# Tying the output product's sums further back, a second partial-sum buffer, and other buffers for the first pair's parts

## The chip, the core and the metric

The kernel runs on one core of a Trainium2 chip. The metric is the device time of one launch in microseconds (us). Five engines work from their own instruction queues: PE (TensorE, the matmuls), ACT (ScalarE), DVE (VectorE), POOL (GpSimd) and SP (SyncE, which here only starts DMAs). The instructions of an engine run in the order in which the program holds them; between engines, semaphores make one wait for another.

## The reference

One decoder block in fp32 on 512 tokens and 16 meta tokens, width 1024: a retention branch and a gated linear-recurrence branch, merged by sigmoid gates, and then a SwiGLU feed-forward part. The change touches the feed-forward part and what shares its helpers:

```python
u = rmsnorm(h, ffn_norm_w[l])
gu = u @ w_ffn_in[l]                      # 1024 x 5632
g, up = gu[..., :FFN_HIDDEN], gu[..., FFN_HIDDEN:]
h = h + (jax.nn.silu(g) * up) @ w_ffn_out[l]   # 2816 x 1024
h = rmsnorm(h, final_norm_w)
```

## The kernel before

**Operands in two parts.** PE multiplies a rounded fp32 type, so each fp32 operand is split into a high part (a cast on ACT) and a low part (source minus high part, on DVE), and each product is three matmuls: high by high, high by low, low by high (lines L431 to L433, or L441 to L443 with 256 columns). For a weight piece of 128x512, `emit` makes the two parts: the cast is L350 (L348 with a sign), the subtraction L356. They live in a ring of 9 buffers, so a piece can be made up to 9 pieces ahead of its use. For an activation `split` does the same (L497 on ACT, L498 on DVE).

**Seven products for eight.** Most products are done in blocks by Winograd's scheme: seven block products of sums and differences of the operands' quarters in place of eight. `fast` and `fast512` do one tile of 128 output columns in that way. They use two PSUM banks, in the trace `zwf` (z and w) and `yxf` (y and x) in the feed-forward part. After the first products of a tile, partial sums are copied out: `ws` (L465, ACT), the second half of `pz` (DVE), the first half of `pz` (L467, ACT); the last product of `yxf`, with the weight sum s2, is added into the bank which L467 has read; then `u2` (L474, ACT) copies the bank and two DVE additions write the tile's output. `pz` has one buffer for each name, so a tile's copy waits for the tile before to have read its own.

**The feed-forward part.** Twenty tiles j = 2 to 21 of `w_fi` (the first two are done in another way ahead of them) give silu(g)*up in 11 pairs of hidden blocks, kept in `F[i]`. `VX` holds the parts of the seven activation operands (t1, t3, b21, b11, ...); at its last use in the last tile, `last_use` gives back an operand's two buffers to `slots`, a list from which `get` takes the one that has been free longest. When the last tile has used t3, `first_parts(0)` starts the output product's first operand.

**The output product** (`fo` in the trace, eight accumulators `acc`, one in each PSUM bank) takes pairs 0 to 8 in two stages, since eight banks hold four of the products at a time. The first stage runs t1, t3, b11, b21 of each pair, 24 matmuls with 512 columns; before each pair's products `first_parts` forms a difference `ab[i]` (L1395, DVE) and splits it and a half of `F[i]`, four casts and subtractions of 128x512. At its end four banks are added out to SBUF (`add_to`, L1490, DVE). The second stage runs t2, b22, t4 of each pair, 18 matmuls. Its operands are begun by `begin_second`: the 128x256 difference L1408, its split, and the difference L1411, all in `F[i]`'s and `ab[i]`'s buffers; `second_parts` splits the other half. The weight sums of t1 and t2 are made in `emit` on DVE (L335 and L337); t3 and t4 come by an adding DMA. Two pairs without Winograd's scheme (9 and 10) fill in after pairs 2 and 5 and end the product, with 48 matmuls at the end; the norm and the writing of the output follow.

**What sets the order.** A scheduler puts the instructions of each engine in an order by its own estimate of when each can start, and the order then is fixed. `behind(ins, other)` adds a dependency that only fixes that ins stands after other on their engine, without a semaphore. `in_turn` ties an addition to the latest low part of a weight (`state["low"]`), and `split(..., held=True)` ties its cast and its subtraction to the latest high and low part, so that an addition can't go ahead of the weights that were emitted before it in the text.

Of the kernel before, what the change touches and what calls it, by code (L numbers as in the profile page):

```python
# [10 lines left out]
F32 = mybir.dt.float32  # L11
F32R = mybir.dt.float32r
# [5 lines left out]
P = 128  # L18
# [37 lines left out]
EARLY = (2, 5)  # L56
BY_DMA = 20
LEAD = 2

ON_POOL = {"w_out": (1, 3)}  # L60
Z_POOL = False
# [96 lines left out]
def hybrid_block(ctx: ExitStack, tc: tile.TileContext, a: dict):  # L158
# [96 lines left out]
    def behind(ins, other):  # L255

        if other is not None:
            tc.add_manual_dep(ins.ins, other.ins.name, mybir.DependencyInfo(
                mybir.DependencyClass.NoSync, mybir.DependencyReason.DATA), reason="issue order")
        return ins  # L260

    def in_turn(ins):
        return behind(ins, state["low"])

    kept = {}
    loaded = {}
# [28 lines left out]
    def emit(n, later=False):  # L295
# [34 lines left out]
        if key == "w_fo" and isinstance(c, str):  # L330
            b11, b12, b21 = (lambda q=q: quarter(key, i, q) for q in (2, 0, 3))
            b22 = lambda: quarter(key, i, 1)
            if c == "t1":
                tb[i] = get(Q4)
                in_turn(nc.vector.tensor_tensor(tb[i], b12(), b11(), op=ALU.add))  # L335
            elif c == "t2":
                in_turn(nc.vector.tensor_tensor(tb[i], tb[i], b22(), op=ALU.add))  # L337
            src = {"t1": lambda: tb[i], "t2": lambda: tb[i], "t4": lambda: tb[i], "t3": lambda: sums[key, i, "t3"],
                   "b11": b11, "b21": b21, "b22": b22}[c]()
        elif c in ("s1", "s2", "s3", "s4"):  # L340
            src = sums[key, i, c]
        else:
            src = quarter(key, i, {"a21": 0, "a22": 1, "a11": 2, "a12": 3}.get(c, c))
# [1 line left out]
        lo = wpool.tile([P, Q4], F32R, tag="lo", bufs=RING, name=f"lo{n}")  # L345
        turned = key == "w_fo" and c == "b11"
        if turned:
            state["high"] = nc.scalar.activation(hi, src, AF.Copy, scale=-1.0)  # L348
        else:
            state["high"] = nc.scalar.copy(hi, src)  # L350
        loaded[pieces[n]] = hi, lo

        def low(engine):
# [6 lines left out]
        if on_pool(key, i, c):  # L360
            low(nc.gpsimd)
        else:
            state["low"] = low(nc.vector)
        if key == "w_fo" and c == "t2":
            add_quarter(tb[i], key, i, 3)
        if key == "w_fo" and c == "t4":
# [79 lines left out]
    def fast(key, s, X, n, banks, name, used):  # L446

        z, w_, y, x = banks
        own = n == TH
        ws = small.tile([P, TH], F32, tag="ws", name=f"ws{name}{s}")
        pz = small.tile([P, 2, TH], F32, tag="pz", name=f"pz{name}{s}")
        u2 = small.tile([P, TH], F32, tag="u2", name=f"u2{name}{s}")
        part = lambda name: weights((key, s, name))[0]
        block(z, part("s1"), X["t1"], n, True)
        used("t1")
        block(w_, part("s3"), X["t3"], n, own)
        used("t3")  # L460
        block(y, part("a12"), X["b21"], n, True)
        used("b21")
        block(x, part("a11"), X["b11"], n, own)
        used("b11")
        nc.scalar.copy(ws[:, :n], w_)  # L465
        nc.vector.tensor_tensor(pz[:, 1, :n], z, ws[:, :n], op=ALU.add)
        nc.scalar.copy(pz[:, 0, :n], x)  # L467
        block(z, part("s4"), X["b22"], n, False)
        used("b22")
        block(w_, part("a22"), X["t4"], n, False)  # L470
        used("t4")
        block(x, part("s2"), X["t2"], n, False)
        used("t2")
        nc.scalar.copy(u2[:, :n], x)  # L474
        return pz, u2
# [19 lines left out]
    def split(p, src, engine=nc.vector, held=False):  # L495
        hi, lo = p
        high = nc.scalar.copy(hi, src)  # L497
        low = engine.tensor_tensor(lo, src, hi.bitcast(F32), op=ALU.subtract)  # L498
        if held:
            behind(high, state["high"])  # L500
            behind(low, state["low"])


    class Pair:
# [883 lines left out]
    def first_parts(i):  # L1388

        if i >= SEVEN or i in parts:  # L1390
            return
        f = F[i]
        ab[i] = get(512)
        by_tile = f.rearrange("p (k n) -> p k n", k=2)
        in_turn(nc.vector.tensor_tensor(ab[i].rearrange("p (k n) -> p k n", k=2), f[:, :512].rearrange("p (k n) -> p k n", k=2),  # L1395
                                by_tile[:, :, 256:], op=ALU.subtract))
        parts[i] = get(D, F32R), get(D, F32R)
        split([p[:, 512:1024] for p in parts[i]], ab[i])
        split([p[:, :512].rearrange("p (k n) -> p k n", k=2) for p in parts[i]], by_tile[:, :, :256], held=True)

# [2 lines left out]
    def begin_second(i):  # L1403

        if i >= SEVEN or i in s2:
            return
        f, t = F[i], ab[i][:, :256]
        in_turn(nc.vector.tensor_tensor(t, f[:, :256], ab[i][:, 256:], op=ALU.subtract))  # L1408
        s2[i] = get(512, F32R)
        split((s2[i][:, :256], s2[i][:, 256:]), t)  # L1410
        nc.vector.tensor_tensor(f[:, 512:768], f[:, 512:768], t, op=ALU.subtract)  # L1411
        put(ab.pop(i))
# [12 lines left out]

    def last_use(b):
        put(*VX.pop(b))
        if b == "t3":
            first_parts(0)

    for j in range(FIRST, NJ):
        gu = get(D)
# [184 lines left out]
```

## Time and profile before

| | |
|---|---|
| three runs | 914.54, 915.37, 916.05 us (median 915.37) |
| the profiled execution | 914.75 us, its span 913.0 us |
| PE busy | 893.9 us of the span (98%), 6506 matmuls |
| DVE busy | 716.3 us (78%) |
| ACT busy | 489.9 us (54%) |
| granted TensorE clock, mean of the span | 0.995 |
| last matmul ends | about 905.3 us after the span's start |

The span is the time from the first to the last instruction of the profiled execution, on whose clock all times below lie. In the timeline a row holds the start, the duration, engine and line, the operation with output and inputs, how many instructions of one kind stand in the row, and in brackets how long the engine had been idle before it and what released it. A matmul's duration overlaps the next one's; the spacing of two starts is what it costs.

### The profile page before, as it was taken

What the parts mean: (1) busy time and instruction counts of PE and PEld (TensorE: products, weight loads), DVE (VectorE), ACT (ScalarE), POOL (GpSimd) and SP (SyncE); (2) the same over time, 40 slices, a digit from 0 to 9 for tenths busy, and PEclk for the clock granted to TensorE, in tenths of its full rate; (3) what the DMA queues carried; (4) which work ended last, traced back from release to release, by engine and by line L of the source; (5) the groups of instructions that cost most, each with busy time, mean ns of one, the idle gap of its engine ahead of it and who ended that gap; (6) DMA issues with size and microseconds to landing.
All of it is one profiled execution on the core that took longest, in us unless ns stands there. A gap on an engine that the chain in (4) does not pass through costs nothing.

```text
span 913.0 us, 17003 instructions
## 1 busy us (share of the span) xinstructions
PE 893.9 (98%) x6506; PEld 843.0 (92%) x6506; DVE 716.3 (78%) x1197; ACT 489.9 (54%) x877; POOL 87.2 (10%) x101
## 2 busy tenths in 40 slices
PE   8999999999999999999999999999999999998996
PEld 7999999999999889999998888999999999886775
DVE  5999978987888738868745427989999997898982
ACT  6655545554466246857833325555565565564553
POOL 3200000000100011211200220000000001101113
PEclk9999999999999999999999999999999999999998
DMA  9723032231234322233443222133333336674512
GB/s 328 203 93 105 26 113 69 93 108 36 81 94 134 108 94 93 70 115 98 140 134 93 92 82 91 48 117 115 94 116 112 98 112 164 191 194 126 125 37 93
DMA packets 53825, 101.26 MB, mean 111 GB/s; under 512 B 6112, under 2 KB 6368, under 8 KB 53744
## 3 DMA queue, kind: packets, MB, share of 16 engines
q1 hardware_dynamic: 48992, 90.43, 31.0%
q0 software_dynamic: 3168, 5.77, 3.8%
q10 hardware_dynamic: 1584, 3.97, 1.4%
q8 instruction: 51, 0.84, 0.4%
q14 instruction: 30, 0.25, 0.1%
HBM read 98.05 MB, written 2.10 MB: 110 GB/s over the span
## 4 chain that ended last, share of the span: by engine, by line
PE 96%; DVE 2%; issue 1%; DMA 1%; ACT 1%; POOL 0%; POOLq 0%; ACTq 0%; DVEq 0%
PE zwf L443 4%; PE zwf L441 4%; PE zwf L442 4%; PE fo L431 4%; PE fo L432 4%; PE fo L433 4%; PE yxf L442 3%; PE yxf L441 3%; PE yxf L443 3%; PE gate L441 2%; PE lg L441 2%; PE lg L443 2%; PE gate L443 2%; PE gate L442 2%; PE lg L442 2%; PE wo L431 2%
## 5 line engine op out<-in xcount | busy, mean ns | idle before, releaser
L356 DVE TENSOR_TENSOR lo<-raw_w_in,hi 128x512 fp32r<-128x512 f32 x99 | 70.7, 719 | 31.2 <-ACT hi L350 29.3
L350 ACT CAST hi<-raw_w_in 128x512 fp32r<-128x512 f32 x99 | 60.8, 620 | 63.7 <-PE w_br L432 13.9
L442 PE MATMUL zwf<-b,hi 128*128 128x256 f32 x320 | 89.3, 279 | 0.0
L443 PE MATMUL zwf<-b,lo 128*128 128x256 f32 x320 | 89.3, 279 | 0.0
L441 PE MATMUL zwf<-b,hi 128*128 128x256 f32 x320 | 89.2, 279 | 0.0
L350 ACT CAST hi<-s_w_fi 128x512 fp32r<-128x512 f32 x80 | 49.8, 622 | 43.7 <-PE zwf L442 37.7
L431 PE MATMUL fo<-hi,b 128*128 128x512 f32 x158 | 62.8, 400 | 4.2 <-ACT b L497 4.2
L442 PE MATMUL yxf<-b,hi 128*128 128x256 f32 x240 | 66.4, 280 | 0.0
L443 PE MATMUL yxf<-b,lo 128*128 128x256 f32 x240 | 66.2, 279 | 0.0
L441 PE MATMUL yxf<-b,hi 128*128 128x256 f32 x240 | 64.2, 279 | 1.3 <-ACT pzf L467 1.3
L350 ACT CAST hi<-raw_w_fi 128x512 fp32r<-128x512 f32 x68 | 41.9, 622 | 39.5 <-PE yxf L442 19.7
L432 PE MATMUL fo<-lo,b 128*128 128x512 f32 x158 | 62.4, 397 | 0.0
L356 DVE TENSOR_TENSOR lo<-s_w_fi,hi 128x512 fp32r<-128x512 f32 x80 | 54.8, 688 | 6.9 <-ACT hi L350 6.5
L443 PEld LDWEIGHTS zwf<-b,lo 128*128 128x128 f32 x320 | 60.2, 188 | 0.0
L441 PEld LDWEIGHTS zwf<-b,hi 128*128 128x128 f32 x320 | 60.2, 188 | 0.0
L442 PEld LDWEIGHTS zwf<-b,hi 128*128 128x128 f32 x320 | 60.1, 188 | 0.0
L497 ACT CAST b<-b 128x512 fp32r<-128x512 f32 (+3 forms) x58 | 39.6, 689 | 34.8 <-DVE b L1168 11.1
L350 ACT CAST hi<-s_w_in 128x512 fp32r<-128x512 f32 x52 | 32.3, 620 | 40.6 <-PE zwgate L442 9.2
L356 DVE TENSOR_TENSOR lo<-raw_w_fi,hi 128x512 fp32r<-128x512 f32 x68 | 46.6, 688 | 6.6 <-ACT hi L350 6.6
L498 DVE TENSOR_TENSOR b<-b,b 128x512 fp32r<-128x512 f32 (+3 forms) x58 | 48.7, 852 | 3.2 <-ACT b L497 3.1
L433 PE MATMUL fo<-hi,b 128*128 128x512 f32 x158 | 47.3, 399 | 1.0 <-DVE b L498 1.0
L356 DVE TENSOR_TENSOR lo<-s_w_in,hi 128x512 fp32r<-128x512 f32 x52 | 35.5, 688 | 12.7 <-ACT hi L350 12.4
(437 smaller groups left out, 3163.9 us busy)
## 6 DMA issues: line engine op xcount, KB each, us to landing
raw_w_in<-in_w_in SPq DMA_DIRECT2D x112, 256.0 KB, 3.0
raw_w_fi<-in_w_fi SPq DMA_DIRECT2D x86, 256.0 KB, 3.1
raw_w_fo<-in_w_fo SPq DMA_DIRECT2D x44, 256.0 KB, 3.8
raw_w_br<-in_w_br SPq DMA_DIRECT2D x16, 256.0 KB, 3.2
raw_w_bl<-in_w_bl SPq DMA_DIRECT2D x16, 256.0 KB, 3.3
raw_w_out<-in_w_out SPq DMA_DIRECT2D x16, 256.0 KB, 2.9
raw_w_v<-in_w_v SPq DMA_DIRECT2D x15, 256.0 KB, 3.5
t_w_fo<-in_w_fo SPq DMA_DIRECT2D x9, 256.0 KB, 3.1
```

The lines of the kernel that those rows point to most:

```text
L350: state["high"] = nc.scalar.copy(hi, src)
L356: return engine.tensor_tensor(lo, src, hi.bitcast(F32), op=ALU.subtract)
L431: nc.tensor.matmul(out, wh, xh, start=start, stop=False, skip_group_check=True)
L432: nc.tensor.matmul(out, wh, xl, start=False, stop=False, skip_group_check=True)
L433: nc.tensor.matmul(out, wl, xh, start=False, stop=stop, skip_group_check=True)
L441: nc.tensor.matmul(out, wh, xh, start=start and i == 0, stop=False, skip_group_check=True)
L442: nc.tensor.matmul(out, wh, xl, start=False, stop=False, skip_group_check=True)
L443: nc.tensor.matmul(out, wl, xh, start=False, stop=i == 3, skip_group_check=True)
L497: high = nc.scalar.copy(hi, src)
L498: low = engine.tensor_tensor(lo, src, hi.bitcast(F32), op=ALU.subtract)
```

## The change

In four places an order or a buffer is set in another way; no instruction is added or removed on any engine.

1. `in_turn` takes a lag and ties to the low part that many places back, not to the latest: 2 back for the weight sums t1 and t2 of `w_fo`, 6 back (`LAG`) for the differences in `first_parts` and `begin_second`. `split(held=True)` ties to the high and the low part 6 back.
2. `pz` has two buffers.
3. When the last tile has used the operand t1, its two buffers go to the front of the list and are taken at once for pair 0's parts (`early`), which `first_parts(0)` uses. Before, pair 0's parts got whichever buffers were first in the list when t3 had been used.
4. Line numbers grow by 3 from L335 on and by up to 8 at the end: L1395, L1408, L1411, L1490, L497 and L498 are L1398, L1411, L1414, L1498, L500 and L501 afterwards.

```diff
--- before.py
+++ after.py
@@ -56,6 +56,7 @@
 EARLY = (2, 5)
 BY_DMA = 20
 LEAD = 2
+LAG = 6
 
 ON_POOL = {"w_out": (1, 3)}
 Z_POOL = False
@@ -259,8 +260,10 @@
                 mybir.DependencyClass.NoSync, mybir.DependencyReason.DATA), reason="issue order")
         return ins
 
-    def in_turn(ins):
-        return behind(ins, state["low"])
+    highs, lows = [], []
+
+    def in_turn(ins, lag):
+        return behind(ins, lows[-lag])
 
     kept = {}
     loaded = {}
@@ -332,9 +335,9 @@
             b22 = lambda: quarter(key, i, 1)
             if c == "t1":
                 tb[i] = get(Q4)
-                in_turn(nc.vector.tensor_tensor(tb[i], b12(), b11(), op=ALU.add))
+                in_turn(nc.vector.tensor_tensor(tb[i], b12(), b11(), op=ALU.add), 2)
             elif c == "t2":
-                in_turn(nc.vector.tensor_tensor(tb[i], tb[i], b22(), op=ALU.add))
+                in_turn(nc.vector.tensor_tensor(tb[i], tb[i], b22(), op=ALU.add), 2)
             src = {"t1": lambda: tb[i], "t2": lambda: tb[i], "t4": lambda: tb[i], "t3": lambda: sums[key, i, "t3"],
                    "b11": b11, "b21": b21, "b22": b22}[c]()
         elif c in ("s1", "s2", "s3", "s4"):
@@ -345,9 +348,9 @@
         lo = wpool.tile([P, Q4], F32R, tag="lo", bufs=RING, name=f"lo{n}")
         turned = key == "w_fo" and c == "b11"
         if turned:
-            state["high"] = nc.scalar.activation(hi, src, AF.Copy, scale=-1.0)
+            highs.append(nc.scalar.activation(hi, src, AF.Copy, scale=-1.0))
         else:
-            state["high"] = nc.scalar.copy(hi, src)
+            highs.append(nc.scalar.copy(hi, src))
         loaded[pieces[n]] = hi, lo
 
         def low(engine):
@@ -360,7 +363,7 @@
         if on_pool(key, i, c):
             low(nc.gpsimd)
         else:
-            state["low"] = low(nc.vector)
+            lows.append(low(nc.vector))
         if key == "w_fo" and c == "t2":
             add_quarter(tb[i], key, i, 3)
         if key == "w_fo" and c == "t4":
@@ -451,7 +454,7 @@
         z, w_, y, x = banks
         own = n == TH
         ws = small.tile([P, TH], F32, tag="ws", name=f"ws{name}{s}")
-        pz = small.tile([P, 2, TH], F32, tag="pz", name=f"pz{name}{s}")
+        pz = small.tile([P, 2, TH], F32, tag="pz", bufs=2, name=f"pz{name}{s}")
         u2 = small.tile([P, TH], F32, tag="u2", name=f"u2{name}{s}")
         part = lambda name: weights((key, s, name))[0]
         block(z, part("s1"), X["t1"], n, True)
@@ -497,8 +500,8 @@
         high = nc.scalar.copy(hi, src)
         low = engine.tensor_tensor(lo, src, hi.bitcast(F32), op=ALU.subtract)
         if held:
-            behind(high, state["high"])
-            behind(low, state["low"])
+            behind(high, highs[-LAG])
+            behind(low, lows[-LAG])
 
 
     class Pair:
@@ -1393,8 +1396,8 @@
         ab[i] = get(512)
         by_tile = f.rearrange("p (k n) -> p k n", k=2)
         in_turn(nc.vector.tensor_tensor(ab[i].rearrange("p (k n) -> p k n", k=2), f[:, :512].rearrange("p (k n) -> p k n", k=2),
-                                by_tile[:, :, 256:], op=ALU.subtract))
-        parts[i] = get(D, F32R), get(D, F32R)
+                                by_tile[:, :, 256:], op=ALU.subtract), LAG)
+        parts[i] = early.pop() if early else (get(D, F32R), get(D, F32R))
         split([p[:, 512:1024] for p in parts[i]], ab[i])
         split([p[:, :512].rearrange("p (k n) -> p k n", k=2) for p in parts[i]], by_tile[:, :, :256], held=True)
 
@@ -1405,7 +1408,7 @@
         if i >= SEVEN or i in s2:
             return
         f, t = F[i], ab[i][:, :256]
-        in_turn(nc.vector.tensor_tensor(t, f[:, :256], ab[i][:, 256:], op=ALU.subtract))
+        in_turn(nc.vector.tensor_tensor(t, f[:, :256], ab[i][:, 256:], op=ALU.subtract), LAG)
         s2[i] = get(512, F32R)
         split((s2[i][:, :256], s2[i][:, 256:]), t)
         nc.vector.tensor_tensor(f[:, 512:768], f[:, 512:768], t, op=ALU.subtract)
@@ -1425,8 +1428,13 @@
 
     def last_use(b):
         put(*VX.pop(b))
+        if b == "t1":
+            slots.free[:] = slots.free[-2:] + slots.free[:-2]
+            early.append((get(D, F32R), get(D, F32R)))
         if b == "t3":
             first_parts(0)
+
+    early = []
 
     for j in range(FIRST, NJ):
         gu = get(D)
```

The scheduler turns these into another order on PE, ACT and DVE: around the retention's third pair of heads (near 183 us), in the gates and the linear recurrence's projections, through the tiles of the feed-forward part, and through the output product. POOL and SP keep theirs. Three places follow, of before and then of the change.

DVE at the end of the output product's first stage. `fo2_1` and the like are accumulators (token tile, half), `lo413` to `lo418` low parts of the weights t2, b22 and t4, `raw_w_fo` weights as loaded, the `b` with 128x256 the second stage's operands. Before:

```order
L356 TENSOR_TENSOR lo415_10337<-b223_9807,hi415_10336 128x512
L1490 TENSOR_TENSOR b158_6329<-b158_6329,fo3_1_9894 128x512
L356 TENSOR_TENSOR lo416_10348<-raw_w_fo0_1_10298,hi416_10347 128x512
L1490 TENSOR_TENSOR b159_6330<-b159_6330,fo0_1_9888 128x512
L1490 TENSOR_TENSOR b160_6331<-b160_6331,fo1_1_9890 128x512
L356 TENSOR_TENSOR lo417_10358<-b218_9713,hi417_10357 128x512
L1408 TENSOR_TENSOR b218_9713<-b187_6947,b218_9713 128x256
L337 TENSOR_TENSOR b224_9913<-b224_9913,raw_w_fo3_1_10374 128x512
L1490 TENSOR_TENSOR b159_6330<-b159_6330,fo2_0_9891 128x512
L1490 TENSOR_TENSOR b160_6331<-b160_6331,fo3_0_9893 128x512
L1411 TENSOR_TENSOR b187_6947<-b187_6947,b218_9713 128x256
L498 TENSOR_TENSOR b247_10368<-b218_9713,b247_10368 128x256
```

With the change:

```order
L1411 TENSOR_TENSOR b218_9713<-b187_6947,b218_9713 128x256
L359 TENSOR_TENSOR lo413_10302<-b218_9713,hi413_10301 128x512
L340 TENSOR_TENSOR b223_9807<-b223_9807,raw_w_fo2_1_10333 128x512
L1411 TENSOR_TENSOR b224_9913<-b191_7177,b224_9913 128x256
L1414 TENSOR_TENSOR b187_6947<-b187_6947,b218_9713 128x256
L359 TENSOR_TENSOR lo414_10323<-b223_9807,hi414_10322 128x512
L1411 TENSOR_TENSOR b227_9971<-b194_7462,b227_9971 128x256
L501 TENSOR_TENSOR b247_10368<-b218_9713,b247_10368 128x256
L1414 TENSOR_TENSOR b191_7177<-b191_7177,b224_9913 128x256
...
L340 TENSOR_TENSOR b224_9913<-b224_9913,raw_w_fo3_1_10374 128x512
L1498 TENSOR_TENSOR b157_6328<-b157_6328,fo2_1_9892 128x512
```

The difference for pair 0 (b218_9713 <- b187_6947), which stood behind four of the bank additions, now stands ahead of all of them, and so do those of pairs 1 and 2, the split of pair 0's (b247) and two of the differences that follow.

ACT from the feed-forward part's last tile into the output product. `hi376` belongs to the last tile's s2, `hi377` to `hi380` to pair 0's t1, t3, b11 and b21, `hi381` on to pair 1; `u2f20`, `wsf21` and `pzf21` are the copies out of the last two tiles; b221 is pair 0's high part. Before:

```order
L348 ACTIVATE hi379_9763<-raw_w_fo0_2_9716 128x512
L350 CAST hi380_9788<-raw_w_fo0_3_9786 128x512
L474 COPY u2f20_9605<-yxf20_9602 128x256
L350 CAST hi381_9813<-b223_9807 128x512
L350 CAST hi382_9832<-t3_w_fo1_9710 128x512
L467 COPY pzf21_9745<-yxf21_9743 128x256
L389 ACTIVATE b219_9738<-b217_9600 128x512
L348 ACTIVATE hi383_9848<-raw_w_fo1_2_9810 128x512
```

With the change:

```order
L500 CAST b221_9763<-b218_9713 128x512
L500 CAST b221_9763<-b187_6947 128x512
L353 CAST hi377_9719<-b218_9713 128x512
L353 CAST hi378_9747<-t3_w_fo0_9638 128x512
L351 ACTIVATE hi379_9765<-raw_w_fo0_2_9716 128x512
L477 COPY u2f20_9605<-yxf20_9602 128x256
L353 CAST hi380_9788<-raw_w_fo0_3_9786 128x512
L500 CAST b225_9915<-b191_7177 128x512
L468 COPY wsf21_9744<-zwf21_9742 128x256
L392 ACTIVATE b219_9738<-b217_9600 128x512
L470 COPY pzf21_9745<-yxf21_9743 128x256
```

Pair 0's two casts to b221 now stand ahead of its weights (before, at the places 749 and 750, behind `u2f21`), and `pzf21` ahead of pair 1's first weights `hi381` and `hi382`.

PE in the last tile (`yxf21`), whose product with b11 (`hi373`) ends here. Before:

```order
L443 MATMUL yxf21_9743<-b165_6340,lo373_9642 128x256
L441 MATMUL yxf21_9743<-b165_6340,hi373_9641 128x256
L442 MATMUL yxf21_9743<-b166_6341,hi373_9641 128x256
L443 MATMUL yxf21_9743<-b165_6340,lo373_9642 128x256
L441 MATMUL yxf21_9743<-b185_6934,hi376_9694 128x256
L442 MATMUL yxf21_9743<-b186_6935,hi376_9694 128x256
L443 MATMUL yxf21_9743<-b185_6934,lo376_9695 128x256
```

With the change:

```order
L446 MATMUL yxf21_9743<-b165_6340,lo373_9642 128x256
L444 MATMUL yxf21_9743<-b165_6340,hi373_9641 128x256
L445 MATMUL yxf21_9743<-b166_6341,hi373_9641 128x256
L446 MATMUL yxf21_9743<-b165_6340,lo373_9642 128x256
L434 MATMUL fo0_1_9888<-hi377_9719,b221_9763 128x512
L435 MATMUL fo0_1_9888<-lo377_9720,b221_9763 128x512
L436 MATMUL fo0_1_9888<-hi377_9719,b222_9764 128x512
```

Eighteen matmuls of pair 0 (t1, t3, b11 into six accumulators) now stand between the last tile's b11 and its s2 (`hi376`), which was next before. Where the second stage begins, PE now runs pair 0's, 1's and 2's t2 into `fo2_1` and `fo3_1` in a row, before pair 0's b22 and t4.

## The prediction

> **What bounds the kernel now.** I read the page first, then the waits of PE, and then the timelines of PE, DVE and ACT around each wait that PE shows late in the span. From the page (engine, busy us and share of the span; the chain of waits; a row of the costliest groups with busy us, mean ns | idle before it and what ended it):
>
> ```profile
> span 913.0 us, 17003 instructions
> ...
> PE 893.9 (98%) x6506; PEld 843.0 (92%) x6506; DVE 716.3 (78%) x1197; ACT 489.9 (54%) x877; POOL 87.2 (10%) x101
> ...
> PE 96%; DVE 2%; issue 1%; DMA 1%; ACT 1%; POOL 0%; POOLq 0%; ACTq 0%; DVEq 0%
> ...
> L350 ACT CAST hi<-s_w_fi 128x512 fp32r<-128x512 f32 x80 | 49.8, 622 | 43.7 <-PE zwf L442 37.7
> ```
>
> PE is the bound. The change keeps its instructions, so time can only come from PE's idle stretches and from matmuls that run slow; it can only be lost to new ones. PE's waits (what waited <- what released it: us in total, times, the longest), without those of the start of the program, which the change leaves as they are:
>
> ```profile
> PE fo L431 <- ACT b L497: 4.2, 3, 3.5
> PE yxf L441 <- ACT pzf L467: 1.3, 1, 1.3
> PE fo L433 <- DVE b L498: 1.0, 2, 0.8
> PE oT L1029 <- DVE b L1093: 0.4, 1, 0.4
> ```
>
> That is 6.9 us of idle time at seven places: one of 3.5 and one of 0.8 where the second stage of the output product begins, two of 0.3 and one of 0.2 later in that stage, 1.3 in the last feed-forward tile, and 0.4 in the retention. All seven lie where the order changes.
>
> **The largest stall, at 837 us.** PE's timeline (start, duration, instruction, count; idle before it in brackets):
>
> ```profile
> 835.83 1.56 PE L433 MATMUL fo<-hi,b 128*128 128x512 f32 x6
> 840.90 0.50 PE L431 MATMUL fo<-hi,b 128*128 128x512 f32 x1 [3.52 <-ACT b L497]
> 841.24 0.40 PE L432 MATMUL fo<-lo,b 128*128 128x512 f32 x1
> ...
> 842.93 1.22 PE L433 MATMUL fo<-hi,b 128*128 128x512 f32 x2 [0.83 <-DVE b L498]
> 843.95 0.63 PE L431 MATMUL fo<-hi,b 128*128 128x512 f32 x1
> ...
> 846.06 0.39 PE L432 MATMUL fo<-lo,b 128*128 128x512 f32 x1
> 846.29 0.39 PE L431 MATMUL fo<-hi,b 128*128 128x512 f32 x1
> ```
>
> Unhindered, two starts lie 0.23 us apart (846.06 to 846.29; I use 0.2325). The six from 835.83 end their starts at 836.99, so the next matmul was due at 837.22 and the one of 846.06, eleven further, at 839.78. It started 6.28 us late. That is more than the idle 4.35 us, since matmuls after the stall ran at half pace. The windows show it (window: its length, then busy us with counts of PE, PEld, DVE, ACT and POOL; then the granted clock, the DMA share, GB/s):
>
> ```profile
> 836.00:846.00 10.00, 5.65 (x17) 3.92 (x17) 10.00 (x20) 3.88 (x8) 1.76 (x2) 0.83 0.45 86
> ...
> 843.00:844.00 1.00, 1.00 (x3) 0.81 (x4) 1.00 (x3) 0.43 (x2) 0.23 (x1) 0.50 0.00 0
> ...
> 846.00:847.00 1.00, 1.00 (x6) 0.75 (x5) 1.00 (x3) 0.95 (x2) 0.00 (x0) 1.00 1.00 229
> ```
>
> Seven steps from 842.93 to 846.06 took 3.13 us where 1.63 was due: 1.50 of the 6.28 us are the granted clock of 0.50.
>
> [...]
>
> Why PE waited stands in the queues of DVE and, last line, ACT:
>
> ```profile
> 835.79 0.69 DVE L1490 TENSOR_TENSOR b<-b,fo 128x512 f32<-128x512 f32 x1 [1.06 <-PE fo L433]
> 836.39 0.68 DVE L356 TENSOR_TENSOR lo<-b,hi 128x512 fp32r<-128x512 f32 x1
> ...
> 838.20 1.28 DVE L1490 TENSOR_TENSOR b<-b,fo 128x512 f32<-128x512 f32 x2
> 839.39 0.68 DVE L356 TENSOR_TENSOR lo<-b,hi 128x512 fp32r<-128x512 f32 x1
> 839.99 0.42 DVE L1408 TENSOR_TENSOR b<-b,b 128x256 f32<-128x256 f32 x1
> ...
> 842.13 0.42 DVE L1411 TENSOR_TENSOR b<-b,b 128x256 f32<-128x256 f32 x1
> 842.46 0.42 DVE L498 TENSOR_TENSOR b<-b,b 128x256 fp32r<-128x256 f32 x1
> ...
> 840.45 0.41 ACT L497 CAST b<-b 128x256 fp32r<-128x256 f32 x1 [3.97 <-DVE b L1408]
> ```
>
> The first operand of t2 (L1408) stood behind four bank additions and three low parts, the first of which could not start before PE had finished a bank; its cast ended at 840.86 and PE went on at 840.90. Its low part L498 stood behind two more bank additions: that is the 0.83.
>
> With the change three L1408, two L1411 and the first L498 stand ahead of the bank additions. A DVE instruction of 512 columns costs 0.60 us in the queue (835.79 to 836.39), one of 256 costs 0.33 (842.13 to 842.46). What stands newly ahead of the first addition is six of 256, two low parts and one weight sum: 6 x 0.33 + 3 x 0.60 = 3.8 us. The cover for it, and for DVE's load as a whole:
>
> ```profile
> 786.00:836.00 50.00, 50.00 (x222) 40.75 (x222) 43.34 (x72) 28.70 (x53) 5.23 (x6) 1.00 0.63 177
> ...
> 786.00:886.00 100.00, 94.79 (x403) 75.28 (x403) 88.49 (x155) 55.12 (x101) 11.37 (x13) 0.98 0.52 133
> ```
>
> DVE is idle for 6.66 us in the first stage, and the ties six back let the differences go into these gaps. PE itself now finishes the bank that the first addition reads 21 matmuls ahead of the first t2: 21 x 0.2325 = 4.9, less 0.4 for the last matmul's end and 0.69 for the addition leaves it 3.8 us early. So one end is no stall (6.28 gained). The other end: only the 1.06 us just ahead of 835.79 can be used. Then the addition starts 2.7 us later than 835.79, PE goes on at 839.2, and 2.0 us are left, which I'd expect without the halved clock (the 1.35 below was followed by none): 4.3 gained. I take the first end, since most of the moved work has its inputs long before, and keep the other for the range.
>
> **The stall at 781 us.** PE, and then ACT:
>
> ```profile
> 781.15 0.28 PE L443 MATMUL yxf<-b,lo 128*128 128x256 f32 x1
> 782.77 0.39 PE L441 MATMUL yxf<-b,hi 128*128 128x256 f32 x1 [1.35 <-ACT pzf L467]
> 783.00 0.28 PE L442 MATMUL yxf<-b,hi 128*128 128x256 f32 x1
> ...
> 781.31 0.62 ACT L350 CAST hi<-b 128x512 fp32r<-128x512 f32 x1 [1.43 <-PE yxf L442]
> 781.84 0.61 ACT L350 CAST hi<-t_w_fo 128x512 fp32r<-128x512 f32 x1
> 782.36 0.37 ACT L467 COPY pzf<-yxf 128x256 f32<-128x256 f32 x1
> ```
>
> 781.15 to 783.00 is 1.85 us where two steps of 0.118 were due: 1.61 lost. The copy that PE needs stood behind two casts for pair 1. Now it stands ahead of them, and PE has 18 matmuls of pair 0 in between, 18 x 0.2325 = 4.2 us. ACT has at most one cast, wsf, the gate's activation and the copy ahead (0.62 + 0.37 + 0.62 + 0.37 = 2.0 by these rows). This gives 1.61 back, if pair 0's operand is there in time. It can be: t1's buffers are free after 12 matmuls of the last tile, and 72 matmuls (8.5 us) follow before the first of pair 0; ACT needs its two casts and three of weights in that time (5 x 0.62 = 3.1), DVE a difference and two subtractions (1.8) beside low parts. The second pz buffer takes away the wait for the tile before; alone it gives nothing, as no row shows a wait on it. Between nothing and 1.61, I take 1.61.
>
> **The small ones.** One of the two rows at 855 and 860 us:
>
> ```profile
> 853.29 1.56 PE L433 MATMUL fo<-hi,b 128*128 128x512 f32 x6
> 855.19 0.50 PE L431 MATMUL fo<-hi,b 128*128 128x512 f32 x1 [0.35 <-ACT b L497]
> 855.53 0.40 PE L432 MATMUL fo<-lo,b 128*128 128x512 f32 x1
> ```
>
> 855.53 was due at 854.92: 0.61 lost with the refill, and twice that is 1.22. The third (1.0 less 0.83, with some refill) is 0.3, the retention's 0.4 with refill 0.5. Between each operand and its use the new order has several products more: PE runs 34 matmuls of 256 columns (4.0 us) ahead of oT, and three t2 in a row start the second stage. Second-stage PE work is 18 x 0.2325 = 4.2 us for a pair against about 4.0 of DVE, so a lead once won isn't eaten up. Bounds: nothing, or all 2.0.
>
> **Sum.** 6.28 + 1.61 + 1.22 + 0.3 + 0.5 = 9.9 us off the profiled execution's 914.75 (its span of 913.0 to 903.1): 904.8. The median of the runs stood 0.6 above it, which gives 905.4.
>
> **The rivals.**
> - DVE is late again (17%). DVE's 88.49 us of work between 786 and 886 now have to fit into 100 - 7.8 = 92.2 us, 96%. If the gaps can't be used, 2.0 us stay at 837 and the small stalls of that stage (1.52) come back: 9.9 - 2.0 - 1.5 = 6.4 off, 909.0. For it speaks the load, against it that DVE's gaps lie ahead of the stall, in the same stage.
> - Pair 0's parts come late (7%). The casts now head ACT's queue and wait for t1's buffers, with the ring's casts and `u2f20` behind them. Then PE waits at pair 0's first product in place of the last tile's: 1.61 stays, 907.0. Against it: 8.5 us for 3.1 us of ACT's work.
> - The change doesn't do what it says (4%): the ties are further back, but t2's weight sum (L337) needs its loaded quarter, and PE stops for that as long as before: 6.28 stays and what is left (3.6) shrinks to less than what can be told, about 914. Against it: these weights' low parts were there before the operand.
> - Slower (6%). In each of the 20 feed-forward tiles ACT's copy `u2f` now stands one cast earlier; it waits for the tile's last product, 12 matmuls or 1.4 us, with weights' casts behind it. If PE then waited for weights, the price is up to 1.4 us a tile; from 0.6 us a tile on (20 x 0.6 = 12) the kernel is slower, and with 0.9 it ends at 905.4 + 18 = 923. Against it: the L350 row of the page, whose casts idle 37.7 us for PE to free a buffer of the ring, so that they run up to eight pieces (8 x 12 x 0.118 = 11 us) ahead.
>
> **How the numbers follow.** The forecast has 66%, its own range 903.6 to 906.8 (0.2 for the clock's estimate and the runs' own spread of 0.8 below; new waits of up to 1.4 above). The range to 909.8 takes in the first two rivals. A change of less than 0.2%, 1.8 us, can't be told from none: faster has 0.90 (the forecast, the first two rivals), same 0.04, slower 0.06.
>
> **What would show it.** In the profile afterwards PE's waits hold none of the four rows above; the window in which the second stage starts has PE at full share with the clock at 1.00; the three differences of `begin_second` lie ahead of the first bank addition; `pzf` of the last tile ends at least 2 us before its user starts. It is wrong if PE's waits name L500 or L501 near the second stage, if DVE stands at full share with PE waiting there, or if `yxf` or `zwf` rows in the tiles show idle time.

## The result and the profile after

The changed kernel takes 905.65 us (median of four runs, 905.58 to 905.80) against 914.95 for the kernel before beside it (four runs, 913.79 to 916.05): a ratio of 0.9899, 95% interval 0.9882 to 0.9916. The forecast was 905.4 within 903.6 to 909.8. The profiled execution took 905.8 us with a span of 903.7; the forecast's own sum had 904.8 and 903.1.

From the page of the changed kernel (span; busy time of the engines):

```profile
span 903.7 us, 16955 instructions
...
PE 892.0 (99%) x6506; PEld 844.8 (93%) x6506; DVE 712.6 (79%) x1197; ACT 489.7 (54%) x877; POOL 88.0 (10%) x101
```

All that PE still waits for in the changed kernel (what waited <- what released it: us, times, longest):

```profile
PE warm L191 <- POOL ident masks.py:199: 2.9, 1, 2.9
PE v L435 <- DVE lo L359: 1.0, 3, 0.4
PE v L434 <- ACT b L672: 0.3, 1, 0.3
PE v L436 <- DVE b L677: 0.2, 1, 0.2
```

These are the program's start, as before. All seven later stalls are gone. At the start of the output product's second stage PE is busy throughout and the clock stays at 1.00, with DVE full (window: length, busy us and counts of PE, PEld, DVE, ACT and POOL, granted clock, DMA share, GB/s); the second row runs from the last feed-forward tile to near the end of the output product:

```profile
836.00:846.00 10.00, 10.00 (x44) 8.11 (x44) 10.00 (x20) 5.61 (x11) 1.75 (x2) 1.00 0.56 119
...
774.00:876.00 102.00, 102.00 (x495) 85.27 (x495) 93.67 (x165) 62.49 (x114) 12.21 (x14) 1.00 0.61 155
```

DVE there, in the changed kernel's timeline:

```profile
827.06 0.41 DVE L1411 TENSOR_TENSOR b<-b,b 128x256 f32<-128x256 f32 x1
...
828.60 0.41 DVE L1411 TENSOR_TENSOR b<-b,b 128x256 f32<-128x256 f32 x1
828.94 0.41 DVE L1414 TENSOR_TENSOR b<-b,b 128x256 f32<-128x256 f32 x1
...
829.88 0.41 DVE L1411 TENSOR_TENSOR b<-b,b 128x256 f32<-128x256 f32 x1
830.21 0.41 DVE L501 TENSOR_TENSOR b<-b,b 128x256 fp32r<-128x256 f32 x1
...
832.69 0.67 DVE L1498 TENSOR_TENSOR b<-b,fo 128x512 f32<-128x512 f32 x1
```

The three differences stand 5.6 to 2.8 us ahead of the first bank addition, which starts without a wait; the end that leaves no stall was the right one. In the 50 us up to 836 us DVE now does 84 instructions and is busy for 48.26 us, where before it did 72 in 43.34:

```profile
786.00:836.00 50.00, 50.00 (x235) 41.48 (x234) 48.26 (x84) 32.35 (x59) 6.10 (x7) 1.00 0.69 190
```

The last tile's copy and its user, from the timelines of ACT and PE of the changed kernel:

```profile
782.66 0.37 ACT L470 COPY pzf<-yxf 128x256 f32<-128x256 f32 x1 [0.56 <-PE yxf L446]
```

```profile
786.65 0.28 PE L444 MATMUL yxf<-b,hi 128*128 128x256 f32 x1
```

The copy ends 3.6 us ahead of the matmul that needs it.

So the step that was forecast happened in full. Yet the profiled execution gained 8.95 us where 9.9 were due, and the pieces show what else happened. The tiles' matmuls run slower; windows of 170 us that hold only tiles, before and then after:

```profile
600.00:770.00 170.00, 170.00 (x1458) 170.00 (x1457) 156.62 (x255) 98.45 (x191) 1.84 (x3) 1.00 0.37 112
```

```profile
600.00:770.00 170.00, 170.00 (x1437) 170.00 (x1436) 153.27 (x252) 96.97 (x189) 1.79 (x2) 1.00 0.37 112
```

1458 matmuls before and 1437 after, PE without a gap and the clock at 1.00 in both: 0.1166 and 0.1183 us for one, and for the tiles' 1680 some 2.9 us more. And the first tile starts at 587.53, not at 589.16 us: 1.63 earlier, of which the retention's stall explains 0.5. The last matmul ends 8.77 us earlier. From the first tile on that is 8.77 - 1.63 = 7.14, which with the 2.9 lost makes 10.0 us won where the stalls had been (9.4 forecast); the tail behind the last matmul shrank by 0.5.

### The profile page after: what moved, and what is told of

Read it like the earlier page. It is cut to its first block, busy times and chain, and to the rows that moved or that the text cites. A ratio compares the mean times of both kernels' runs of the same rounds, so it can differ in the third digit from the quotient of the medians.

```text
span 903.7 us, 16955 instructions
## 1 busy us (share of the span) xinstructions
PE 892.0 (99%) x6506; PEld 844.8 (93%) x6506; DVE 712.6 (79%) x1197; ACT 489.7 (54%) x877; POOL 88.0 (10%) x101
## 4 chain that ended last, share of the span: by engine, by line
PE 97%; DVE 1%; DMA 1%; ACT 1%; issue 0%; POOL 0%; POOLq 0%; ACTq 0%; DVEq 0%
PE zwf L444 4%; PE zwf L446 4%; PE zwf L445 4%; PE fo L436 4%; PE fo L435 4%; PE fo L434 4%; PE yxf L445 3%; PE yxf L444 3%; PE yxf L446 3%; PE gate L446 2%; PE lg L446 2%; PE lg L445 2%; PE gate L445 2%; PE lg L444 2%; PE gate L444 2%; PE wo L436 2%
## 5 line engine op out<-in xcount | busy, mean ns | idle before, releaser
L445 PE MATMUL yxf<-b,hi 128*128 128x256 f32 x240 | 67.6, 282 | 0.0
L444 PE MATMUL yxf<-b,hi 128*128 128x256 f32 x240 | 67.4, 281 | 0.0
L435 PE MATMUL fo<-lo,b 128*128 128x512 f32 x158 | 59.2, 394 | 0.0
L434 PE MATMUL fo<-hi,b 128*128 128x512 f32 x158 | 57.5, 393 | 0.0
L436 PE MATMUL fo<-hi,b 128*128 128x512 f32 x158 | 56.1, 394 | 0.0
L500 ACT CAST b<-b 128x512 fp32r<-128x512 f32 (+3 forms) x58 | 39.2, 689 | 27.6 <-DVE b L1171 11.6
L501 DVE TENSOR_TENSOR b<-b,b 128x512 fp32r<-128x512 f32 (+3 forms) x58 | 48.7, 847 | 3.4 <-ACT b L500 3.3
L445 PEld LDWEIGHTS yxf<-b,hi 128*128 128x128 f32 x240 | 45.2, 188 | 0.0
```

The costliest lines, as they stand in the source:

```text
L434: nc.tensor.matmul(out, wh, xh, start=start, stop=False, skip_group_check=True)
L435: nc.tensor.matmul(out, wh, xl, start=False, stop=False, skip_group_check=True)
L436: nc.tensor.matmul(out, wl, xh, start=False, stop=stop, skip_group_check=True)
L444: nc.tensor.matmul(out, wh, xh, start=start and i == 0, stop=False, skip_group_check=True)
L445: nc.tensor.matmul(out, wh, xl, start=False, stop=False, skip_group_check=True)
```

## The experiments

All times are medians, with the lowest and the highest run in brackets where they matter; ratios are to the kernel before beside the run, with their 95% interval. In the edits, `...` stands for lines left out.

**Only the second pz buffer.** The changed kernel with the ties and pair 0's buffers put back:

```diff
-        return behind(ins, lows[-lag])
+        return behind(ins, lows[-1])
...
-            behind(high, highs[-LAG])
-            behind(low, lows[-LAG])
+            behind(high, highs[-1])
+            behind(low, lows[-1])
...
-        if b == "t1":
-            slots.free[:] = slots.free[-2:] + slots.free[:-2]
-            early.append((get(D, F32R), get(D, F32R)))
```

> Only the second pz buffer is changed, the ties and pair 0's buffers are as before. Theory A (the second buffer alone reorders the feed-forward tiles, and that order makes their matmuls start 1.5% further apart): the stalls at the start of the second stage and behind it stay (6.28 + 1.22 + 0.3), the retention's 0.4 goes, the last tile's stall shrinks, and the 1680 matmuls of the tiles take some 2.9 us longer; time 914.5 to 916. Rival B (the pace in the tiles is the chip's or the run's, or belongs to another part of the change): the tiles run at 0.1165 us a matmul as before, time 912 to 913.2.

Measured: 915.07 us, ratio 1.0006 (0.9996 to 1.0016). PE's waits in this run, and its tiles:

```profile
PE fo L434 <- ACT b L500: 4.5, 4, 3.5
...
PE yxf L444 <- ACT pzf L470: 0.5, 1, 0.5
```

```profile
600.00:770.00 170.00, 170.00 (x1437) 170.00 (x1436) 153.35 (x252) 97.07 (x188) 1.80 (x2) 1.00 0.36 112
```

The retention's wait is gone and the last tile's shrank to 0.5, but the tiles run at the slow pace. Alone this part is worth nothing: what it wins is paid back in the tiles.

**Only the ties.** The changed kernel with one pz buffer and without pair 0's buffers:

```diff
-        pz = small.tile([P, 2, TH], F32, tag="pz", bufs=2, name=f"pz{name}{s}")
+        pz = small.tile([P, 2, TH], F32, tag="pz", name=f"pz{name}{s}")
...
-        if b == "t1":
-            slots.free[:] = slots.free[-2:] + slots.free[:-2]
-            early.append((get(D, F32R), get(D, F32R)))
```

> Only the ties are moved back, pz has one buffer and pair 0's parts take the buffers they took before. Theory A (each stall has its own cause): the stalls of the output product go (6.28 + 1.22 + 0.3 = 7.8), the 1.6 in the last tile stays or grows to 2.8, the retention's 0.4 stays, the tiles keep 0.1165 us a matmul: 907.2 to 908.6. Rival B (the pace in the tiles belongs to the ties): 910 to 911.

Measured: 908.77 us (908.06 to 910.49), ratio 0.9942 (0.9927 to 0.9957). The profile is that of the slowest of the four runs:

```profile
PE yxf L444 <- ACT pzf L470: 2.1, 1, 2.1
...
PE zwf L444 <- DVE pzf L469: 0.5, 1, 0.5
PE oT L1032 <- DVE b L1096: 0.4, 1, 0.4
```

No wait of `fo` is left: the ties alone clear the output product. The last tile's stall grows, to 2.1 and 0.5 us. Behind it the clock falls, for 6.8 us by these windows (from 784.8 to 791.6) where it was 3.4 us in the kernel before:

```profile
781.00:783.00 2.00, 0.19 (x2) 0.00 (x0) 2.00 (x4) 1.35 (x4) 0.87 (x1) 1.00 0.87 289
783.00:785.00 2.00, 1.71 (x12) 1.49 (x12) 2.00 (x4) 0.92 (x3) 0.00 (x0) 0.94 0.83 174
785.00:787.00 2.00, 1.47 (x7) 1.44 (x7) 2.00 (x5) 1.69 (x4) 0.00 (x0) 0.50 0.62 161
787.00:789.00 2.00, 2.00 (x11) 2.00 (x11) 2.00 (x4) 0.97 (x3) 0.45 (x1) 0.50 0.52 168
789.00:791.00 2.00, 2.00 (x11) 2.00 (x11) 1.92 (x4) 0.58 (x2) 0.41 (x1) 0.50 0.67 152
791.00:793.00 2.00, 2.00 (x9) 1.62 (x8) 1.91 (x4) 1.55 (x3) 0.00 (x0) 0.85 0.88 217
```

The tiles keep 1458 matmuls in 170 us, so theory A holds for the pace; the time is 0.2 over its range, which had no term for the halved clock. The runs differ in time as they do in mean clock: 0.998 at 908.06, 0.997 at 908.35, 0.996 at 909.19 and 0.994 at 910.49 us.

**Only pair 0's buffers.** One pz buffer, and the ties put back as in the first run:

```diff
-        return behind(ins, lows[-lag])
+        return behind(ins, lows[-1])
...
-        pz = small.tile([P, 2, TH], F32, tag="pz", bufs=2, name=f"pz{name}{s}")
+        pz = small.tile([P, 2, TH], F32, tag="pz", name=f"pz{name}{s}")
...
-            behind(high, highs[-LAG])
-            behind(low, lows[-LAG])
+            behind(high, highs[-1])
+            behind(low, lows[-1])
```

> Only pair 0's parts are placed in t1's buffers. Theory A: the last tile's stall of 1.6 goes and nothing else, time 913.2 to 913.8, the second stage begins with the same 3.5 and 0.8 us of waits. Rival B (the 1.6 go only with the second pz buffer): 914.5 to 915.3.

Measured: 913.85 us, ratio 0.9991 (0.9982 to 1.0001). Its waits of PE:

```profile
PE fo L434 <- ACT b L500: 4.5, 4, 3.5
...
PE fo L436 <- DVE b L501: 1.0, 2, 0.8
PE oT L1032 <- DVE b L1096: 0.4, 1, 0.4
```

The wait on `pzf` is gone with one pz buffer, so it is this part that clears the last tile; one more wait of 0.3 us has come up in the second stage. In time the interval just touches no change, and the median lies 0.05 us above theory A's range; in the trace it is theory A.

**Without the second pz buffer.**

```diff
-        pz = small.tile([P, 2, TH], F32, tag="pz", bufs=2, name=f"pz{name}{s}")
+        pz = small.tile([P, 2, TH], F32, tag="pz", name=f"pz{name}{s}")
```

> The change without the second pz buffer. Theory A (that buffer is not needed for the last tile's stall, and its order costs the tiles 2.9 us): all stalls but the retention's 0.4 go, the tiles keep 0.1165 us a matmul, what the second buffer's order gained ahead of the tiles (1.6 us) is lost: 904.0 to 905.2, faster than with the whole change. Rival B (the pace is not from that buffer): the tiles run at 0.1183 and the time is 906.8 to 908.

Measured: 904.70 us (904.25 to 904.97), ratio 0.9894 (0.9879 to 0.9909). Waits and tiles:

```profile
PE oT L1032 <- DVE b L1096: 0.4, 1, 0.4
```

```profile
600.00:770.00 170.00, 170.00 (x1458) 170.00 (x1457) 156.83 (x255) 98.43 (x190) 1.80 (x2) 1.00 0.37 111
```

0.95 us less than the whole change, though the retention's wait is back. (The intervals of the two ratios overlap, since the kernel before scatters; the runs of the two kernels themselves, 904.25 to 904.97 and 905.58 to 905.80, don't. They were not taken side by side, but the kernel before beside them took 914.83 and 914.95.) The ties and pair 0's buffers carry the gain.

Which of the two slows the tiles: the order of their matmuls, which the second buffer changes, or the place of the buffers behind it? The activations' buffers (4224 bytes a partition each) follow the partial sums by the order of the pools in kernel.py, so another pz of 2112 bytes moves all of them. The next two runs cross the two.

**The old order at the new places.** Without the second buffer, but with a pad of its size:

```diff
+    pad = small.tile([P, 2, TH], F32, tag="pad", name="pad")
+    nc.gpsimd.memset(pad[:, 0, :1], 0.0)
...
-        pz = small.tile([P, 2, TH], F32, tag="pz", bufs=2, name=f"pz{name}{s}")
+        pz = small.tile([P, 2, TH], F32, tag="pz", name=f"pz{name}{s}")
```

> The change without the second pz buffer, and 2112 bytes a partition left empty ahead of the activations' buffers (with one memset of 4 bytes a partition on POOL): the order of PE, DVE and ACT is that of the run without the second buffer, the addresses of the activations' buffers are those of the whole change. Theory A (the order of the tiles' products sets the pace): tiles at 0.1168 us a matmul, 904.4 to 905.2. Rival B (the addresses that the second buffer shifts set it): tiles at 0.1185, 1680 x 0.00175 = 2.9 us more: 907.2 to 908.2.

Measured: 906.06 us (905.77 to 906.73), ratio 0.9910 (0.9893 to 0.9926).

```profile
600.00:770.00 170.00, 170.00 (x1436) 170.00 (x1435) 155.06 (x251) 96.86 (x188) 1.80 (x2) 1.00 0.37 111
```

The tiles are slow (1436) with the order that was fast: rival B, and theory A falls. The time lies 1.1 us under rival B's range, since the same shift makes the stages ahead of the tiles faster. The first matmul of the k projection and the first of the tiles, without the pad and then with it:

```profile
41.29 0.29 PE L444 MATMUL k<-b,hi 128*128 128x264 f32 x1
...
589.62 0.28 PE L444 MATMUL zwf<-b,hi 128*128 128x256 f32 x1
```

```profile
40.69 0.29 PE L446 MATMUL k<-b,hi 128*128 128x264 f32 x1
...
587.84 0.28 PE L446 MATMUL zwf<-b,hi 128*128 128x256 f32 x1
```

548.33 us against 547.15: 1.18 less for the same instructions in the same order.

**The new order at the old places.** The whole change, with pz behind the activations' buffers and the pad in its place:

```diff
+    sums_pool = ctx.enter_context(tc.tile_pool(name="sums_pool", bufs=1))
...
+    pad = small.tile([P, 2, TH], F32, tag="pad", name="pad")
+    nc.gpsimd.memset(pad[:, 0, :1], 0.0)
...
-        pz = small.tile([P, 2, TH], F32, tag="pz", bufs=2, name=f"pz{name}{s}")
+        pz = sums_pool.tile([P, 2, TH], F32, tag="pz", bufs=2, name=f"pz{name}{s}")
```

> The whole change, with the two pz buffers placed behind the activations' buffers and 2112 empty bytes in their old place: the tiles' order is that of the whole change, the addresses of the activations' buffers are those of the kernel before. Theory A (order): tiles at 0.1185 us a matmul, 905.3 to 906.2. Rival B (addresses): tiles at 0.1168, 902.4 to 903.4.

Measured: 904.85 us (904.54 to 905.13), ratio 0.9894 (0.9879 to 0.9909).

```profile
600.00:770.00 170.00, 170.00 (x1448) 170.00 (x1447) 154.51 (x254) 98.02 (x190) 1.94 (x3) 1.00 0.37 112
```

In between, in time and in pace, so neither theory has it alone. The order costs something too: 1458 to 1448 at the old places, nothing more at the new ones (1436 and 1437).

**Two pz buffers everywhere but in the tiles.**

```diff
-        pz = small.tile([P, 2, TH], F32, tag="pz", bufs=2, name=f"pz{name}{s}")
+        pz = small.tile([P, 2, TH], F32, tag="pzf" if name == "f" else "pz", bufs=1 if name == "f" else 2, name=f"pz{name}{s}")
```

> The whole change with two pz buffers everywhere but in the feed-forward tiles, which have one of their own: their order is that of the run without the second buffer, the retention and the gates have the order of the whole change; the activations' buffers lie 4224 bytes higher than before. Theory A (order): tiles at 0.1168, the retention's 0.4 gone and the 1.1 us won ahead of the tiles kept: 902.4 to 903.6. Rival B (addresses): with a shift of 4224 rather than 2112 either pace is possible, 902.8 or 905.7; read together with the two runs beside it.

Measured: 903.19 us (903.16 to 903.39), ratio 0.9876 (0.9861 to 0.9891).

```profile
600.00:770.00 170.00, 170.00 (x1462) 170.00 (x1462) 156.21 (x256) 98.97 (x191) 2.67 (x3) 1.00 0.37 113
```

This is 2.5 us less than the whole change. No wait of PE's is left behind the start, and the tiles are as fast as ever, with everything 4224 bytes higher. The time lies in theory A's range, but rival B allowed it too; what the run shows is that a shift as such is not slow. 2112 is 16 times 128 and 64 more, 4224 a whole multiple of 128; since the buffers are a multiple of 128 long, all of them start at the same place within 128 bytes: by the author's estimate 96 in the kernel before and here, 32 in the changed one. (The 96 is worked out from the sizes in kernel.py of the buffers ahead of them, and so are the shifts; no trace has addresses, and the differences between the runs need the shifts alone.) The next runs test that on this version.

**Pads of 32, 64, 96 and 1024 bytes.** Each is the version above with a pad, of 8, 16, 24 or 256 columns; this is the one with 16, 64 bytes:

```diff
+    pad = small.tile([P, 16], F32, tag="pad", name="pad")
+    nc.gpsimd.memset(pad[:, :1], 0.0)
```

> The whole change with one pz buffer for the tiles (903.2), and the activations' buffers 32 bytes a partition higher; the orders are the same. Theory A (what counts is where an activation's buffer starts within 128 bytes: 96 was fast at 9.78 and 9.81 us a tile, 32 slow at 9.96): the start is now 0, which none of the runs had, so the tiles may take another time than 9.78, anything from 9.6 to 10.0. Rival B (it is the place in kilobytes): 9.78 us a tile, 903.2.

> As the run beside it with 64 bytes. Theory A: the start is 32 within 128 bytes, as in the whole change, and the tiles take 9.93 to 9.97 us, 3 us more in all, about 905 with what the stages ahead win by it (1.2). Rival B: 9.78 us a tile, 903.2.

> As the runs with 32, 64 and 1024 bytes, with 96: the start is 64 within 128 bytes, the one of the four residues in steps of 32 that no run had. Theory A (only 96 is fast): the tiles take 9.9 to 10.0 us as at 0 and 32, the time is 904.5 to 907. Rival B (64 is fast as well, or 0 alone and 32 are slow for another reason): 9.78 us a tile or less, 902.5 to 903.5.

> As the two beside it with 1024 bytes. Theory A: the start is 96 within 128 bytes as without the pad, 9.77 to 9.79 us a tile and 903.0 to 903.4. Rival B (the place in kilobytes counts): another time for a tile, as the shifts of 2112 and 4224 gave 9.96 and 9.78.

Measured: 907.28, 905.34, 906.81 and 902.95 us (ratios 0.9922, 0.9900, 0.9919 and 0.9875; the last 0.9858 to 0.9891). The tiles, in the order of 32, 64, 96 and 1024:

```profile
600.00:770.00 170.00, 170.00 (x1439) 170.00 (x1439) 155.84 (x253) 96.95 (x188) 1.80 (x2) 1.00 0.37 111
```

```profile
600.00:770.00 170.00, 170.00 (x1434) 170.00 (x1433) 154.55 (x250) 97.19 (x189) 2.20 (x3) 1.00 0.37 112
```

```profile
600.00:770.00 170.00, 170.00 (x1443) 170.00 (x1443) 155.86 (x253) 97.31 (x188) 1.80 (x2) 1.00 0.37 111
```

```profile
600.00:770.00 170.00, 170.00 (x1462) 170.00 (x1462) 156.17 (x256) 98.83 (x191) 2.66 (x3) 1.00 0.38 113
```

Theory A each time, though with 32 bytes it allowed nearly any pace, and the last time lies 0.05 us under its range. With the tiles in this one order, they are fast with a shift of 0, 4224 or 5248 bytes, multiples of 128 (1458 to 1462; a start of 96 by the estimate), and slow with 32, 64 and 96 bytes over a multiple (1439, 1434 to 1436, 1443; starts of 0, 32 and 64). Four bytes cleared by POOL at the start can't be it, since the last run has them too. The stretch ahead, from the k projection's first matmul to the tiles' first, took 548.19, 546.27, 548.10 and 547.83 us, and 547.81 without a pad: it is fastest with the pad of 64, a start of 32. The version with 1024 is the fastest of the study; its runs (902.83 to 903.03) lie just under those without the pad.

**Only begin_second's tie.** Of the whole change this one line stays:

```diff
-LAG = 6
+W_LAG, F_LAG, S_LAG, H_LAG = 1, 1, 6, 1
...
-        in_turn(nc.vector.tensor_tensor(t, f[:, :256], ab[i][:, 256:], op=ALU.subtract), LAG)
+        in_turn(nc.vector.tensor_tensor(t, f[:, :256], ab[i][:, 256:], op=ALU.subtract), S_LAG)
```

with W_LAG for the weight sums, F_LAG in first_parts and H_LAG in split, one pz buffer, and without pair 0's buffers.

> Of the whole change only begin_second's difference is tied six low parts back; the weight sums, first_parts, the held splits, pz and pair 0's buffers are as before. Theory A (the differences alone are not what is late; DVE is full for 10.00 of the 10 us around 840, and what they overtake comes late in its turn): the 3.5 us stop turns into several of at most 1.5, the granted clock stays at 1.00, so that the 1.5 us of slow matmuls and 0.5 to 1.5 of idle time are won: 911.8 to 913. Rival B (the place of these differences is the whole cause): the 4.35 us of idle time and the 1.5 go, 908 to 909.

Measured: 910.91 us (910.65 to 911.20), ratio 0.9962 (0.9947 to 0.9977), between the two. Waits, and two windows (same columns as above):

```profile
PE yxf L444 <- ACT pzf L470: 1.3, 1, 1.3
PE fo L434 <- ACT b L500: 1.2, 1, 1.2
PE fo L436 <- DVE b L501: 0.8, 1, 0.8
```

```profile
836.00:846.00 10.00, 8.00 (x31) 5.82 (x30) 10.00 (x20) 4.48 (x10) 1.99 (x3) 0.93 0.47 85
840.00:850.00 10.00, 8.00 (x27) 5.79 (x26) 10.00 (x20) 6.22 (x12) 2.63 (x3) 0.83 0.56 111
```

The 3.5 and 0.8 us at the second stage's start became 1.2 and 0.8, somewhat later, and the small waits behind them are gone. DVE is still full, and now a low part (0.8 us) and then a high part (1.2) come late. This is theory A's mechanism, several shorter stops, but it won more idle time than theory A gave it, and the clock still halved (0.83 over ten us), which theory A had denied. The other ties, which let DVE work ahead in the first stage, are needed for the rest: with all of them nothing is left.

## Why the prediction was right, and where it was not

- **All seven stalls go, worth 9.9 us.** They went. The single runs show whose doing it was: the output product's by the ties, the last tile's by pair 0's buffers, the retention's by the second pz buffer. The choice between the two ends at 837 us (no stall, or 2.0 left) was right, for the reason given: DVE did the moved work in the first stage's gaps.
- **"The change keeps its instructions, so time can only come from PE's idle stretches and from matmuls that run slow; it can only be lost to new ones."** This step failed. No new idle stretch came, and the tiles still lost 2.9 us to a slower pace at full clock. The second pz buffer moves the activations' buffers by 2112 bytes, and this move alone costs all of it (1436 matmuls in the old order); the second buffer's order alone costs nearly half (1448 at the old places), and on top of the move nothing. The same move won 1.1 to 1.2 us in the stages ahead, and the order 0.6 to 0.7 (the whole change's 587.53 - 41.00 = 546.53 us there is 1.80 less than without that buffer). Of this only the retention's 0.5 was in the sum. Besides, the stretches where the stalls had been gave 0.6 us more than forecast, and the tail 0.5. These gains and the 2.9 us lost largely cancelled; none of them was in the sum, so that it still fits is luck.
- **"The second pz buffer takes away the wait for the tile before; alone it gives nothing."** Its run gave nothing (1.0006), but not for the reason given: it took the retention's wait away, shortened the last tile's and made the stages ahead faster, and lost as much in the tiles.
- **2.0 us of stall without the halved clock.** Not borne out: a stall of 2.10 us was followed by 0.50 for 6.8 us, and in the single tie's run so were one of 0.8 and one of 1.2 close together, while the 1.35 of the kernel before was not. On this evidence the clock's cost belongs into the price of a stall of two microseconds here. The price of the largest stall, too, was that of one execution: the run with only the second pz buffer has the same stop of 3.5 us, and its clock fell during the stop and stayed at 0.50 for about twice as long (the last section has the rows).
- **The median 0.6 above the profiled execution.** It was carried over from the kernel before, and afterwards the median lies 0.15 below. The profiled executions alone moved by 8.95 us, 1.0 less than the sum; this offset made the forecast of the median look better than its parts. What lay behind the offset seems to have gone with the stalls, though no run shows it by itself: the kernel before ran with mean clocks of 0.993 to 0.997 and spread over 2.3 us, the changed one with 0.998 and 0.2 us.
- **The range.** Its lower bound of 903.6 lies 1.8 under the forecast, but the two terms named for it (0.2 and 0.8) reach only 904.4. No run shows the 0.2 for the clock's estimate; what the runs showed in its place is a clock at 0.50 for 3.4 us in the kernel before (842.6 to 846.0, 1.50 us lost) and for 6.8 us with the ties alone; with the change it stays at 1.00 from 836 to 850 us. The upper bound of the forecast's own range follows from its term.
- **The rivals.** None came in its own way. The slower one, the tiles paying for the new order, was looked for in waits of the weights' casts, and there were none; the tiles did pay, a quarter of its threshold (2.9 of 12 us), by another mechanism.

What stays open is why the tiles slow down when the buffers move by other than a multiple of 128 bytes. The share differs by product (in the kernel before one of a tile's seven products ran at 0.113 us a matmul, 618.31 to 619.67 us for 12, and the others at 0.117 to 0.118), the idle share of PE is zero in both, and no run took reads of the moving operand apart from the loading of weights, or from what ACT, DVE and the DMA queues do in the same buffers. The small buffers between the pad and the activations' (the copies `u2` among them) moved along in these runs; no matmul of the kernel reads the partial sums, so the activations' are the likelier ones, but that is argued, not shown. Nor was it tried whether another start is better for the stages ahead of the tiles and for the tiles at once, though 32 was the fastest for the former and 96 for the latter. Nor were the weight sums', the first stage's and the held splits' ties tried one by one.

## What to carry to other kernels

Tie an instruction that prepares the next stage's operand to work some places back, not to the latest, and see in the trace whether the engine has gaps ahead of the stall into which it can go. Judge each part of a change by its own run: here the part that the gain didn't need cost about a microsecond, and a change that only adds a buffer moves every buffer behind it. Where PE has no idle time, compare matmuls per window: a pace that is 1.5% worse (1437 in 170 us for 1458 here) shows in no list of waits.

## What the runs showed of the hardware

- The pace of back-to-back matmuls with 256 columns changed with where the activations' buffers lie in SBUF: with the tiles' instructions in the same order, 1458 to 1462 in 170 us with a shift of 0, 4224 or 5248 bytes against the kernel before (multiples of 128, by the sizes in kernel.py), and 1434 to 1443 with 2112, 4256, 4288 or 4320 (64, 32, 64 and 96 over a multiple). Ahead of the tiles 64 over a multiple was faster (547.15 against 548.33 us in one order, 546.27 against 547.81 in the other).
- The granted clock fell to 0.50 after a stall of 2.10 us (at about 784.8 us, for 6.8 us, with the ties alone) and after two of 0.81 and 1.20 us close together (between 844 and 845 us, for 3.4 us by the ten from 840, with begin_second's tie alone). After one of 1.35 us in the kernel before it stayed at 1.00 (781 to 789 us).
- What a stall costs in clock varied between executions: one kernel ran 908.06 us at a mean clock of 0.998 and 910.49 at 0.994. The moment of the fall differed between two kernels with the same stop. In the kernel before, the clock held through the 3.52 us stop, which ended at 840.90, and fell only at about 842.6, in the next, shorter one; it stayed low for about 3.4 us. With only the second pz buffer it fell at about 839.8, during the same stop (3.5 us), and stayed low for about twice as long (by the means below 0.11 x 30 / 0.50 = 6.6 us, against 0.06 x 30 / 0.50 = 3.6). The two windows in which it fell, each with the mean of the 30 us around it, of the kernel before and of the run with the second buffer:

```profile
842.00:843.00 1.00, 0.17 (x2) 0.07 (x1) 1.00 (x4) 1.00 (x3) 0.00 (x0) 0.80 0.02 8
830.00:860.00 30.00, 24.96 (x100) 18.92 (x98) 27.45 (x52) 15.27 (x30) 6.04 (x7) 0.94 0.55 131
```

```profile
838.00:840.00 2.00, 0.00 (x0) 0.00 (x0) 2.00 (x4) 0.00 (x0) 0.46 (x1) 0.94 0.40 62
830.00:860.00 30.00, 26.00 (x99) 19.66 (x97) 27.25 (x52) 15.18 (x29) 5.80 (x7) 0.89 0.58 131
```

What sets the moment of the fall was not shown.
